# Both MLPs' down-projections computed token by token, summed in SBUF over four blocks, and turned once by PE transposes

## The chip, the core and the metric

The kernel runs on one core of a Trainium2 chip. A core has a matrix engine (TensorE, "PE" in the profile) that multiplies a stationary block of up to 128x128, loaded first, with a moving block of up to 512 columns and writes the sums to banks of PSUM; a vector engine (VectorE, DVE), a scalar engine (ScalarE, ACT), GpSimd (POOL), and a queue engine (SyncE, SP) that issues transfers from device memory. The operands lie in SBUF, 128 partitions wide. Each engine works through its own instructions in order and waits for the others by semaphores.

The metric is the device time of one execution in microseconds, median over the runs shown.

## The reference, cut to what matters

The model is a decoder trunk of two layers over 256 tokens with 2048 features: an attention mixer, an MLP with squared ReLU, and a gate with a per-layer embedding. What the change touches is the MLP of both layers, and through it the residual stream `h` that the gate's norm reads:

```python
hn = rmsnorm(h, mlp_norm_g[i])
h = h + jnp.square(jax.nn.relu(hn @ mlp_w1[i])) @ mlp_w2[i]
gate = jax.nn.sigmoid(rmsnorm(h, ple_norm_g[i]) @ ple_w_gate[i])
h = h + (p[i] @ ple_w_proj[i]) * gate
```

`mlp_w1[i]` is 2048 x 8192 and `mlp_w2[i]` 8192 x 2048, all float32. Every product is made from split numbers: each operand is a rounded part (hi) and the rest (lo), and hi x hi, hi x lo and lo x hi are summed.

## The kernel before

**Layout.** Activations are kept feature-major: tile `x[k]` holds features 128k to 128k+127 on the partitions and the 256 tokens along the free axis; two such tiles are one buffer `xp[j]`. A split activation (`xa`, `h`) is a tile of 512 columns, hi for 256 tokens and then lo for the same tokens.

**Weights.** They stream from device memory in chunks of 128x1024 float32, 512 KB each. For each chunk SyncE issues a load to `raw`, ScalarE casts it to `whi` (L196), VectorE subtracts to make `wlo` (L202). `Program.run` writes the order of all this out by hand, one step a chunk: first loads, casts and subtractions for chunks some steps ahead, then `advance`, which moves every open follow-up generator by one `yield`, and then the matmuls of the chunk. A generator that yields `"tensor"` is resumed behind the chunk's matmuls (`finish_tensor`), so that it can put work of its own on TensorE there. Each engine gets its instructions in just this order.

**The quad (L341).** A chunk of the MLP holds 256 input features times 512 output features. `quad` computes four feature-major output tiles at once, in four PSUM banks. For each of the four and each of the two inner blocks, `mm_tile` (L316) takes 128x128 of weights as the stationary operand: hi weights against the 512 columns of the activation (its hi and lo part together, L318), then lo weights against 256 columns (the hi part, L319). These two are called a pair below; a chunk is 8 pairs. The two halves of a bank have to be added afterwards. Banks come from two rings, "mm" with four single banks and "at" with two double ones, and `parity` alternates between them.

**The token-major unit (L384).** The value projections of both mixers use another form: the activation block is stationary and 512 columns of weights move, once each for hi x hi, lo x hi and hi x lo (L401 to L403). Output is token-major, 128 tokens by 512 features, in two banks, one for each half of the tokens, with no halves to add. A chunk is 12 matmuls of 512 columns.

**The MLP (L452).** The hidden width is cut into four blocks of 2048. For each block `b` four quads (the "up stage", 32 chunks) compute the block's hidden tiles `h`, then four quads (the "down stage", 32 chunks) multiply them with `w2`. After each down quad `done` adds the two halves of its four banks straight into `x[k]`, by two vector additions of 256 columns a tile (`add_to_x`, L433), in every block. In the last block it goes on with `renorm` (L302): split the new `x[k]` for the gate (L289 on ScalarE, L293 on VectorE), square it (L218) and sum the squares (L226) for the gate's norm.

**What follows.** `ple` (L489) alternates a projection quad of one chunk with a gate quad of eight. During the first gate quad, from its fifth chunk on, `Norm.factor` waits for all 16 tiles, sums the squares over partitions by four one-column matmuls (`column`, L234), takes root and inverse, and spreads the result over the partitions by two float32 products of 256 columns (`spread`, L257); the same is done in the first up quad of an MLP for its own norm.

Of the kernel before, what the change touches and what calls it, by code (L numbers as in the profile page):

```python
# [10 lines left out]
F32 = mybir.dt.float32  # L11
# [4 lines left out]
P = 128  # L16
D = 2048
T = 256
KT = D // P
# [9 lines left out]
NFB = 4  # L29
# [7 lines left out]
G_ATTN, G_MLP, G_PLE, G_KV, G_FIN = 0, 2, 4, 6, 7  # L37
# [94 lines left out]
def kernel(ctx: ExitStack, tc: tile.TileContext, a: dict, out: bass.AP):  # L132
    nc = tc.nc
# [11 lines left out]
    cur = {}  # L145
# [10 lines left out]
    def bank():  # L156
        return pspool.tile([P, 512], F32, tag="mm", name="mm", bufs=4)

    def banks2():
        return pspool.tile([P, 2, 512], F32, tag="at", name="at", bufs=2)  # L160
# [4 lines left out]
    xp = [xpool.tile([P, 2 * T], F32, name=f"x{j}") for j in range(KT // 2)]  # L165
# [3 lines left out]
    ident = const.tile([P, P], F32, name="ident")  # L169
# [117 lines left out]
    def split_hi(k, gi):  # L287
        t = xap.tile([P, 2 * T], F32R, tag="xa", name="xa")
        nc.scalar.activation(t[:, :T], x[k], AF.Identity, scale=gains[:, gi, k:k + 1])  # L289
        return t  # L290

    def split_lo(t, k, gi):
        nc.vector.scalar_tensor_tensor(t[:, T:], x[k], gains[:, gi, k:k + 1], f32(t[:, :T]),  # L293
                                       op0=ALU.mult, op1=ALU.subtract)
# [7 lines left out]
    def renorm(k, gi, to, norm):  # L302

        t = split_hi(k, gi)
        s = norm.square(k)
        yield
        split_lo(t, k, gi)
        to[k] = t
        norm.add(s)


    def have(acts, k):
        prog.until(lambda: acts[k] is not None)
        return acts[k]

    def mm_tile(ps, hi, lo, col, rhs, first, last):  # L316

        nc.tensor.matmul(ps, hi[:, col:col + P], rhs, start=first, stop=False)  # L318
        nc.tensor.matmul(ps[:, :T], lo[:, col:col + P], rhs[:, :T], start=False, stop=last)  # L319

    def sum_halves(ps):
        s = tmp.tile([P, T], F32, tag="es", name="es", bufs=4)
        nc.scalar.copy(s, ps[:, :T])  # L323
        t = tmp.tile([P, T], F32, tag="et", name="et", bufs=7)
        nc.vector.tensor_add(t, ps[:, T:], s)  # L325
        return t

    parity = [0]

    def four_banks():  # L330
        parity[0] ^= 1
        if parity[0]:
            return [bank() for _ in range(4)]
        return [p[:, i, :] for p in (banks2(), banks2()) for i in range(2)]

    def delayed(g, n):
        for _ in range(n):
            yield
        yield from g

    def quad(src, nk, acts, done, hooks=None, single_ring=False, late=False):  # L341

        st = []
        for c in range(nk // 2):
            def step(hi, lo, c=c):
                if c == 0:
                    st.extend([bank() for _ in range(4)] if single_ring else four_banks())
                for i in range(2):
                    have(acts, 2 * c + i)
                for f in range(4):  # L350
                    for i in range(2):
                        k = 2 * c + i
                        mm_tile(st[f], hi, lo, i * 512 + f * P, acts[k], k == 0, k == nk - 1)
                if c < nk // 2 - 1:
                    return []
                return [delayed(done(f, st[f]), f // 2 if late else 0) for f in range(4)]
            prog.chunk(src(c), step)
            for fn in (hooks or {}).get(c, ()):
                prog.op(fn)
# [21 lines left out]
                for fn in mid:  # L381
                    prog.op(fn)

    def token_major(src, acts, done, hooks=None, ring=bank):  # L384

        st = []
        for c in range(KT // 2):
            def step(hi, lo, c=c):
                if c == 0:
                    if ring is bank:  # L390
                        st.extend([bank(), bank()])
                    else:
                        b = banks2()
                        st.extend([b[:, 0, :], b[:, 1, :]])
                for i in range(2):
                    k = 2 * c + i
                    xg = have(acts, k)
                    wh, wl = hi[:, i * 512:(i + 1) * 512], lo[:, i * 512:(i + 1) * 512]
                    for j in range(2):
                        xh, xl = xg[:, j * P:(j + 1) * P], xg[:, T + j * P:T + (j + 1) * P]  # L400
                        nc.tensor.matmul(st[j], xh, wh, start=k == 0, stop=False)  # L401
                        nc.tensor.matmul(st[j], xl, wh, start=False, stop=False)  # L402
                        nc.tensor.matmul(st[j], xh, wl, start=False, stop=k == KT - 1)  # L403
                return [done(j, st[j]) for j in range(2)] if c == KT // 2 - 1 else []
            prog.chunk(src(c), step)
            for fn in (hooks or {}).get(c, ()):
                prog.op(fn)
# [20 lines left out]
    def split_to(dst, src):  # L428
        nc.scalar.copy(dst[:, :T], src)
        yield  # L430
        nc.vector.tensor_sub(dst[:, T:], src, f32(dst[:, :T]))

    def add_to_x(k, ps):  # L433
        nc.vector.tensor_add(x[k], ps[:, :T], x[k])
        nc.vector.tensor_add(x[k], ps[:, T:], x[k])
# [14 lines left out]
                prog.op(lambda: parity.__setitem__(0, 1))  # L450

    def mlp(layer, xg, norm, to, norm2):  # L452
        for b in range(NFB):
            h = [None] * 16
            for q in range(4):
                def done(f, ps, q=q, h=h):
                    t = sum_halves(ps)
                    yield
                    while norm.r is None:
                        yield  # L460
                    nc.vector.scalar_tensor_tensor(t, t, 0.0, norm.rb, op0=ALU.max, op1=ALU.mult)
                    yield
                    nc.scalar.activation(t, t, AF.Square)
                    ht = cur["h"].tile([P, 2 * T], F32R, tag="h", name="h", bufs=20)
                    yield from split_to(ht, t)
                    h[4 * q + f] = ht
                base = layer * 128 + (b * 4 + q) * 8
                quad(lambda c, base=base: a["w1"][base + c], KT, xg, done,
                     {4: [norm.factor]} if b == 0 and q == 0 else None, late=True)
            for q in range(4):  # L470
                def done(f, ps, q=q, b=b):
                    k = 4 * q + f
                    add_to_x(k, ps)
                    if b == NFB - 1:
                        yield
                        yield from renorm(k, G_PLE + layer, to, norm2)
                base = layer * 128 + (b * 4 + q) * 8
                quad(lambda c, base=base: a["w2"][base + c], 16, h, done, late=True)

    def load_p(layer, to):  # L480
        for k in range(2):
# [99 lines left out]
    def start_x(k):  # L581
        return split_x(k, G_ATTN, x_a0)
# [22 lines left out]
    def qk_done(h, i, ps):  # L605
        if i == 0:
            qk[h] = cur["A"].tile([P, 6 * T], F32, tag="qk", name="qk", bufs=2)
            ready[h] = 0

        def mark():  # L610
            ready[h] += 1
        yield from to_head(ps, n_a0, qk[h][:, i * T:(i + 1) * T], True, mark)
# [84 lines left out]
    def v_unit(u, hooks=None, ring=bank):  # L697
        token_major(lambda c: a["w_v"][u * 8 + c], x_a0, lambda j, ps: v_done(u, j, ps), hooks, ring)

    hooks = {c: [lambda k=k: start_x(k) for k in (2 * c + 2, 2 * c + 3)] for c in range(7)}  # L700
# [3 lines left out]
    for h in range(HA):  # L704
        for i in range(6):
            single(lambda c, h=h, i=i: a["w_qk"][(h * 6 + i) * 2 + c], x_a0,
                   lambda ps, h=h, i=i: qk_done(h, i, ps),
# [19 lines left out]
    p0, p1 = [None] * 2, [None] * 2  # L727
    prog.op(lambda: load_p(0, p0))
    mlp(0, x_m0, n_m0, x_p0, n_p0)
    ple(0, p0, x_p0, n_p0, x_kv, n_b1, False)  # L730

# [394 lines left out]
    for h in range(HB):  # L1126
# [4 lines left out]
        if h:  # L1131
            prog.op(lambda h=h: b_scores(h - 1))
    hooks = {0: [lambda: b_pv(HB - 4, True), lambda: b_transpose(HB - 3)],
             1: [lambda: b_scores(HB - 1, banks2)],
             2: [lambda: b_pv(HB - 3, True), lambda: b_transpose(HB - 2)],
             4: [lambda: b_pv(HB - 2, True), lambda: b_transpose(HB - 1)],
             5: [lambda: b_pv(HB - 1, True)]}
# [3 lines left out]
    prog.op(lambda: open_pool("h"))  # L1141
    prog.op(lambda: load_p(1, p1))
    mlp(1, x_m1, n_m1, x_p1, n_p1)
    ple(1, p1, x_p1, n_p1, None, n_fin, True)

# [99 lines left out]
```

## Time and profile before

| | us |
|---|---|
| median of 3 runs | 2523.98 (2523.86 to 2524.05) |
| the profiled execution | 2523.56 |
| its span, first to last instruction | 2521.8 |
| a down stage (32 chunks) | 88.75 |
| an up stage that is not the first of its layer | 88.74 |
| TensorE busy in the span | 2502.3 |

Times of a profile are microseconds from the span's start unless a column says ns. PE is TensorE's matmul, PEld its weight load. A line such as `L318 PE MATMUL mm<-h,whi` names a source line, engine, operation, and the tiles written and read; "mm" and "at" are the two rings of banks. Busy time of PE counts overlapping latencies, so the distance between starts says more than a duration. PEclk is the granted clock of TensorE as a share of full speed.

### The profile page before, as it was taken

Reading aid. Unit: us, or ns where it says so; the run is one execution under the profiler, and the core shown is the slowest. Engines: PE = TensorE matmul, PEld = TensorE weight load, DVE = VectorE, ACT = ScalarE, POOL = GpSimd, SP = SyncE. Lnnn points to the kernel's source line nnn. Section 1 sums busy time; section 2 is a strip of 40 time slices with the busy share of each in tenths; the row PEclk is TensorE's granted clock in tenths of the full one; section 3 lists DMA queues with packets and bytes.
Section 4 is the critical chain, followed back from the end, with each engine's and each line's share of the span. In section 5 each row is a group of like instructions: output and inputs, shape, how many; then the busy total and the mean of one; then the engine's idle time right before and its main releaser. Section 6 shows DMA issues by size and latency. Waiting matters only on the chain.

```text
span 2521.8 us, 37917 instructions
## 1 busy us (share of the span) xinstructions
PE 2502.3 (99%) x14399; PEld 2198.0 (87%) x14399; DVE 1719.2 (68%) x3005; ACT 1339.7 (53%) x2146; POOL 10.4 (0%) x24
## 2 busy tenths in 40 slices
PE   9999999999999999999999999999999999999997
PEld 7888888888888888888888889888888888888887
DVE  6766677866566665567787989776656556556777
ACT  6444444554354453455564788655435445445555
POOL 0000000000000000000000000000000000000000
PEclk9999999999999999999999999999999999999999
DMA  7555555566666666566566754456666666666663
GB/s 265 175 177 180 172 164 177 176 187 191 189 189 191 192 187 191 191 190 187 186 198 191 243 159 125 142 189 186 191 191 189 189 190 191 190 189 191 191 185 118
DMA packets 129831, 466.23 MB, mean 185 GB/s; under 512 B 14576, under 2 KB 15600, under 8 KB 129648
## 3 DMA queue, kind: packets, MB, share of 16 engines
q1 hardware_dynamic: 128400, 461.76, 58.7%
q8 instruction: 113, 1.85, 0.3%
q0 software_dynamic: 528, 1.07, 0.2%
q10 hardware_dynamic: 720, 0.98, 0.1%
q14 instruction: 70, 0.57, 0.1%
HBM read 461.65 MB, written 2.10 MB: 184 GB/s over the span
## 4 chain that ended last, share of the span: by engine, by line
PE 99%; DVE 1%; DMA 0%; issue 0%; ACT 0%; SPq 0%; DVEq 0%
PE mm L318 31%; PE at L318 26%; PE mm L319 16%; PE at L319 13%; PE mm L403 1%; PE mm L401 1%; PE mm L402 1%; PE at L401 1%; PE at L402 1%; PE at L403 1%; PE at L1092 0%; PE at L635 0%; PE mm L1116 0%; PE mm L855 0%; PE mm L856 0%; PE mm L688 0%
## 5 line engine op out<-in xcount | busy, mean ns | idle before, releaser
L202 DVE TENSOR_TENSOR wlo<-raw,whi 128x1024 fp32r<-128x1024 f32 (+1 forms) x874 | 1065.1, 1220 | 623.6 <-PE at L319 242.1
L196 ACT CAST whi<-raw 128x1024 fp32r<-128x1024 f32 (+1 forms) x874 | 920.3, 1054 | 914.6 <-PE at L318 407.7
L318 PE MATMUL mm<-xa,whi 128*128 128x512 f32 x2176 | 766.4, 396 | 0.0
L319 PE MATMUL mm<-xa,wlo 128*128 128x256 f32 x2176 | 608.8, 280 | 0.0
L318 PE MATMUL at<-xa,whi 128*128 128x512 f32 x1648 | 573.6, 392 | 0.0
L318 PEld LDWEIGHTS mm<-xa,whi 128*128 128x128 f32 x2176 | 407.9, 187 | 92.6 <-issue 0.4
L319 PE MATMUL at<-xa,wlo 128*128 128x256 f32 x1648 | 461.1, 280 | 0.0
L319 PEld LDWEIGHTS mm<-xa,wlo 128*128 128x128 f32 x2176 | 410.8, 189 | 0.4
L318 PEld LDWEIGHTS at<-xa,whi 128*128 128x128 f32 x1648 | 308.3, 187 | 68.0
L318 PE MATMUL mm<-h,whi 128*128 128x512 f32 x1024 | 355.7, 391 | 0.0
L318 PE MATMUL at<-h,whi 128*128 128x512 f32 x1024 | 355.7, 391 | 0.0
L319 PEld LDWEIGHTS at<-xa,wlo 128*128 128x128 f32 x1648 | 311.3, 189 | 0.1
L319 PE MATMUL mm<-h,wlo 128*128 128x256 f32 x1024 | 286.7, 280 | 0.0
L319 PE MATMUL at<-h,wlo 128*128 128x256 f32 x1024 | 286.7, 280 | 0.0
L318 PEld LDWEIGHTS at<-h,whi 128*128 128x128 f32 x1024 | 191.5, 187 | 42.0
L318 PEld LDWEIGHTS mm<-h,whi 128*128 128x128 f32 x1024 | 191.5, 187 | 42.0
L319 PEld LDWEIGHTS mm<-h,wlo 128*128 128x128 f32 x1024 | 193.5, 189 | 0.0
L319 PEld LDWEIGHTS at<-h,wlo 128*128 128x128 f32 x1024 | 193.5, 189 | 0.0
L325 DVE TENSOR_TENSOR et<-mm,es 128x256 f32<-128x256 f32 x137 | 55.7, 421 | 83.0 <-ACT es L323 80.9
L323 ACT COPY es<-mm 128x256 f32<-128x256 f32 x137 | 48.3, 371 | 67.5 <-PE mm L319 64.6
L325 DVE TENSOR_TENSOR et<-at,es 128x256 f32<-128x256 f32 x103 | 43.4, 422 | 36.7 <-ACT es L323 31.2
L323 ACT COPY es<-at 128x256 f32<-128x256 f32 x103 | 37.7, 370 | 51.8 <-DVE et L325 40.3
(292 smaller groups left out, 2372.3 us busy)
## 6 DMA issues: line engine op xcount, KB each, us to landing
raw<-in_w SPq DMA_DIRECT2D x512, 512.0 KB, 3.5
raw<-in_w_qk SPq DMA_DIRECT2D x96, 512.0 KB, 3.6
raw<-in_w_gate SPq DMA_DIRECT2D x56, 512.0 KB, 3.6
raw<-in_w_kv SPq DMA_DIRECT2D x48, 512.0 KB, 4.2
raw<-in_w_v SPq DMA_DIRECT2D x47, 512.0 KB, 3.6
raw<-in_w_q SPq DMA_DIRECT2D x32, 512.0 KB, 4.3
raw<-in_w_oB SPq DMA_DIRECT2D x32, 512.0 KB, 3.6
raw<-in_w_oA SPq DMA_DIRECT2D x16, 512.0 KB, 3.6
```

The source lines that it names most:

```text
L196: nc.scalar.copy(hi[:, c], t[:, c])
L202: nc.vector.tensor_sub(lo[:, c], t[:, c], f32(hi)[:, c])
L318: nc.tensor.matmul(ps, hi[:, col:col + P], rhs, start=first, stop=False)
L319: nc.tensor.matmul(ps[:, :T], lo[:, col:col + P], rhs[:, :T], start=False, stop=last)
L323: nc.scalar.copy(s, ps[:, :T])
L325: nc.vector.tensor_add(t, ps[:, T:], s)
L401: nc.tensor.matmul(st[j], xh, wh, start=k == 0, stop=False)
L402: nc.tensor.matmul(st[j], xl, wh, start=False, stop=False)
L403: nc.tensor.matmul(st[j], xh, wl, start=False, stop=k == KT - 1)
```

## The change

The down stages become token-major units. For each block and each quarter `q` of the output features a unit multiplies the stationary `h` blocks with the moving weights into two banks. `token_major` gets a parameter `whole`: banks alternate between the two rings, and one follow-up serves both token halves. The follow-up `down` adds the banks to a new token-major tile `y` of 256 x 2048 float32 in SBUF: in block 0 ScalarE copies them there, in blocks 1 to 3 VectorE adds them. In the last block it goes on, one `yield` a chunk: behind the second chunk after the unit, eight PE transposes of 128x128 turn the quarter's columns of `y` into two banks of the other ring; then two additions of 512 columns put them into `xp`, and two rounds of `renorm` follow for two tiles each. The loads, their order and the split of the weights stay as they were. The attention mixers' value units use the same helper as before.

```diff
-    def token_major(src, acts, done, hooks=None, ring=bank):
+    def two_banks(mm):
+        if mm:
+            return [bank(), bank()]
+        b = banks2()
+        return [b[:, 0, :], b[:, 1, :]]
+
+    def token_major(src, acts, done, hooks=None, ring=bank, whole=False):
 
         st = []
         for c in range(KT // 2):
             def step(hi, lo, c=c):
                 if c == 0:
-                    if ring is bank:
-                        st.extend([bank(), bank()])
+                    if whole:
+                        parity[0] ^= 1
+                        st.extend([parity[0], two_banks(parity[0])])
+                        st[:] = st[1] + st[:1]
                     else:
-                        b = banks2()
-                        st.extend([b[:, 0, :], b[:, 1, :]])
+                        st.extend(two_banks(ring is bank))
...
-                return [done(j, st[j]) for j in range(2)] if c == KT // 2 - 1 else []
+                if c < KT // 2 - 1:
+                    return []
+                return [done(*st)] if whole else [done(j, st[j]) for j in range(2)]
...
     def mlp(layer, xg, norm, to, norm2):
+
+        def down(b, q, ps0, ps1, mm):
+            c = slice(q * 512, (q + 1) * 512)
+            if b == q == 0:
+                cur["y"] = cur["h"].tile([P, 2, D], F32, name=f"y{layer}")
+            y = cur["y"]
+            for j, ps in enumerate((ps0, ps1)):
+                if b:
+                    nc.vector.tensor_add(y[:, j, c], ps, y[:, j, c])
+                else:
+                    nc.scalar.copy(y[:, j, c], ps)
+            if b < NFB - 1:
+                return
+            yield
+            yield "tensor"
+            tr = two_banks(not mm)
+            for f in range(4):
+                for j in range(2):
+                    k = 4 * q + f
+                    nc.tensor.transpose(tr[f // 2][:, (f % 2 * 2 + j) * P:(f % 2 * 2 + j + 1) * P],
+                                        y[:, j, k * P:(k + 1) * P], ident)
+            yield
+            for i in range(2):
+                nc.vector.tensor_add(xp[2 * q + i], tr[i], xp[2 * q + i])
+            for i in range(2):
+                yield
+                both = [renorm(4 * q + 2 * i + f, G_PLE + layer, to, norm2) for f in range(2)]
+                for g in both:
+                    next(g)
+                yield
+                for g in both:
+                    next(g, None)
+
         for b in range(NFB):
...
             for q in range(4):
-                def done(f, ps, q=q, b=b):
-                    k = 4 * q + f
-                    add_to_x(k, ps)
-                    if b == NFB - 1:
-                        yield
-                        yield from renorm(k, G_PLE + layer, to, norm2)
                 base = layer * 128 + (b * 4 + q) * 8
-                quad(lambda c, base=base: a["w2"][base + c], 16, h, done, late=True)
+                token_major(lambda c, base=base: a["w2"][base + c], h,
+                            lambda ps0, ps1, mm, b=b, q=q: down(b, q, ps0, ps1, mm), whole=True)
```

In the changed kernel the three matmuls of the token-major unit are lines L408 to L410, and the transposes are L481.

## The prediction

> **What bounds the kernel now.** I read the page's busy times first, then its chain, then the groups of instructions, to see which engine sets the end and which lines it spends its time on.
>
> ```profile
> span 2521.8 us, 37917 instructions
> ...
> PE 2502.3 (99%) x14399; PEld 2198.0 (87%) x14399; DVE 1719.2 (68%) x3005; ACT 1339.7 (53%) x2146; POOL 10.4 (0%) x24
> ...
> PE 99%; DVE 1%; DMA 0%; issue 0%; ACT 0%; SPq 0%; DVEq 0%
> PE mm L318 31%; PE at L318 26%; PE mm L319 16%; PE at L319 13%; PE mm L403 1%; PE mm L401 1%; PE mm L402 1%; PE at L401 1%; PE at L402 1%; PE at L403 1%; PE at L1092 0%; PE at L635 0%; PE mm L1116 0%; PE mm L855 0%; PE mm L856 0%; PE mm L688 0%
> ...
> L318 PE MATMUL mm<-h,whi 128*128 128x512 f32 x1024 | 355.7, 391 | 0.0
> L318 PE MATMUL at<-h,whi 128*128 128x512 f32 x1024 | 355.7, 391 | 0.0
> ```
>
> The end is set by TensorE alone: the chain is 99% PE, 86% of it in the matmul pairs of L318 and L319, and these groups show no idle time before them. The 391 ns are latencies of overlapping matmuls; what counts is how far apart they start. So every term below is a count of matmuls times a distance between starts. The 2 x 1024 groups on h are the 256 chunks that the change rewrites (8 pairs a chunk, 32 chunks in each of 8 down stages). I then took the stretches: a down stage, the up stage behind it, and a token-major value unit of mixer A, which already runs the three matmuls that the down stages will get.
>
> ```profile
> core 0: us, PE busy (x) PEld busy (x) DVE busy (x) ACT busy (x) POOL busy (x), PEclk, DMA share, GB/s
> 581.63:670.38 88.75, 88.75 (x515) 78.25 (x513) 52.90 (x70) 37.27 (x43) 0.00 (x0) 1.00 0.61 191
> 670.38:759.12 88.74, 88.74 (x514) 78.24 (x513) 53.81 (x75) 46.80 (x70) 0.00 (x0) 1.00 0.61 190
> 64.83:86.62 21.79, 21.79 (x98) 18.03 (x97) 18.21 (x40) 8.86 (x11) 0.00 (x0) 1.00 0.50 164
> ```
>
> A stage of 32 chunks takes 88.75 us, 2.773 us a chunk, without a gap and at full clock (counts include neighbours that reach into a window). The eight chunks of the token-major unit take 21.79 us, 2.724 a chunk, at the same clock.
>
> **The change part by part.** *The matmuls.* A chunk had 8 matmuls of 512 columns and 8 of 256; it gets 12 of 512. That is 6144 columns either way, but four instructions fewer. The distances stand in the timeline, fast pairs first, then the end of a token-major unit and the pairs behind it (columns: start, duration, instruction).
>
> ```profile
> 758.08 0.39 PE L318 MATMUL at<-xa,whi 128*128 128x512 f32 x1
> 758.31 0.28 PE L319 MATMUL at<-xa,wlo 128*128 128x256 f32 x1
> 758.43 0.39 PE L318 MATMUL at<-xa,whi 128*128 128x512 f32 x1
> ...
> 759.12 0.39 PE L318 MATMUL mm<-h,whi 128*128 128x512 f32 x1
> ```
> ```profile
> 85.71 0.39 PE L403 MATMUL mm<-wlo,xa 128*128 128x512 f32 x1
> ...
> 86.39 0.39 PE L403 MATMUL mm<-wlo,xa 128*128 128x512 f32 x1
> 86.62 0.39 PE L318 MATMUL mm<-xa,whi 128*128 128x512 f32 x1
> ...
> 86.96 0.40 PE L318 MATMUL mm<-xa,whi 128*128 128x512 f32 x1
> ...
> 87.31 0.40 PE L318 MATMUL mm<-xa,whi 128*128 128x512 f32 x1
> ...
> 87.67 0.40 PE L318 MATMUL mm<-xa,whi 128*128 128x512 f32 x1
> ...
> 88.02 0.40 PE L318 MATMUL mm<-xa,whi 128*128 128x512 f32 x1
> ```
>
> A fast pair takes 0.3467 us (88.75 / 256); three token-major matmuls take 0.68 (85.71 to 86.39), 0.2267 each. A chunk falls from 8 x 0.3467 = 2.773 to 12 x 0.2267 = 2.720, so 256 chunks save 256 x 0.0533 = 13.6 us. The unit's 21.79 is 0.03 above 8 x 2.72: its first matmuls are slower. A later unit, behind a slower stretch of pairs, took 0.06 more than 21.76:
>
> ```profile
> 283.51:305.33 21.82, 12.48 (x32) 5.89 (x32) 1.00 0.65 194
> ```
>
> Eight such entries give back 0.4.
>
> The rule of the Trainium skill, "TensorE: Matmul & The Clock Gate", section "Back-to-back issue gap", that a warm matmul takes its columns over 2.4 GHz plus 2.5 ns, speaks against the change. By it four fewer matmuls are worth 10 ns a chunk, 2.6 us in all (an estimate from that page); the trace disagrees, at 227 ns where the rule has 216 and 347 for a pair where it has 325.
>
> *The transposes.* In the last block of each layer every quarter turns 8 blocks of 128x128, so 64 in all, on PE's path between two chunks. Mixer A has nine of them inside a token-major unit:
>
> ```profile
> 439.85 0.27 PE L663 MATMUL at<-ident,p 128*128 128x128 f32 x1
> 439.95 0.27 PE L664 MATMUL at<-ident,p 128*128 128x128 f32 x1
> ...
> 440.50 0.49 PE L666 MATMUL mm<-ident,p 128*128 128x128 f32 x3
> 440.75 0.47 PE L401 MATMUL mm<-whi,xa 128*128 128x512 f32 x1
> 441.06 0.39 PE L402 MATMUL mm<-whi,xa 128*128 128x512 f32 x1
> ...
> 441.52 0.40 PE L401 MATMUL mm<-whi,xa 128*128 128x512 f32 x1
> ```
>
> From 439.85 to 441.52 are nine transposes and three matmuls: 1.67 - 0.68 = 0.99, or 0.11 each. Eight cost 0.88, with a little unrest behind them 0.9; eight groups cost 7.2 us (bounds 7.0 to 7.7).
>
> *The pairs behind a token-major unit.* This is the term that the diff hides. Above, the pairs after 86.62 start 0.34, 0.35, 0.36, 0.35 apart, not 0.347: the stream falls into a slower rhythm, and stays in it.
>
> ```profile
> core 0: us, PE busy (x) PEld busy (x), PEclk, DMA share, GB/s
> 30.14:55.53 25.39, 25.39 (x72) 13.34 (x71) 1.00 0.68 222
> 86.67:95.10 8.43, 8.43 (x24) 4.32 (x23) 1.00 0.72 254
> 146.60:155.08 8.48, 8.46 (x24) 4.32 (x23) 1.00 0.52 181
> 245.18:253.66 8.48, 8.47 (x24) 4.32 (x23) 1.00 0.53 179
> 305.38:313.86 8.48, 8.47 (x24) 4.32 (x23) 1.00 0.62 186
> ```
>
> These windows hold L318 alone behind the five whole value units of mixer A (two open 0.05 late, to leave a neighbour out). 25.44 / 72 and 8.48 / 24 are both 0.3533 a pair, five times of five, with no return until something else comes between. In the MLP each down stage but the last is followed by an up stage of 256 pairs. Today those follow pairs and run at 0.3466; behind token-major matmuls each should take 256 x 0.0067 = 1.71 us longer, and six of them 10.2 us. Bounds: 0, if the fast rhythm comes back at once, and 10.2. I take 10.2, because the nearest rows agree to the nanosecond and the exit state is the same.
>
> *The end of a layer.* The last quarter's work now takes add, transposes, add, and two rounds of splits: by the generator's steps the last input of the gate is ready seven chunks after the quarter's end instead of four, and is needed in the ninth. This hides behind two chunks, 5.5 us; if the cover went, TensorE would wait 2.8 us a chunk. The last transposes are queued behind the gate's first chunk and wait for the projection's banks, which come free some 2 us into that chunk of 2.8 (an estimate: four copies and an addition of about 0.4 each); it too hides. All of the gate's matmuls are queued behind them. The additions from the transposed banks wait on the vector engine, with the next chunk's subtraction behind them, four chunks early. What shows is the slow rhythm: projection and six chunks of the gate, 7 x 8 pairs x 0.0067 = 0.37 a layer, less 0.05 since the norm's column sums move one chunk later; both layers 0.6 (bounds 0 and 0.8). The two wide products of the norm's spread put the stream right:
>
> ```profile
> 1228.43 0.59 PE L257 MATMUL mm<-diag,ones 128*128 128x256 f32 x2
> 1228.67 0.58 PE L318 MATMUL mm<-pg,whi 128*128 128x512 f32 x1
> ...
> 1229.56 0.39 PE L318 MATMUL mm<-pg,whi 128*128 128x512 f32 x1
> ...
> 1229.90 0.39 PE L318 MATMUL mm<-pg,whi 128*128 128x512 f32 x1
> ```
>
> *Other engines, at nothing.*
>
> ```profile
> L434 DVE TENSOR_TENSOR x<-at,x 128x256 f32<-128x256 f32 x80 | 33.3, 417 | 2.1
> L620 ACT ACTIVATE v<-mm,col x10: 680/690/692, 87.5 to 443.8; 128x512 fp32r<-128x512 f32 x5, 128x512 f32<-128x512 f32 x5
> ```
>
> Per stage 32 additions of 0.42 us go and 8 wide ones of about 0.7 (an estimate, from the ScalarE row of that width) come, so VectorE's 52.9 of 88.75 falls; in block 0 ScalarE gets 8 copies of 0.69, on 37.3 of 88.75. The queue of loads keeps its order; a chunk of 512 KB in 2.72 us asks 193 GB/s, where a stretch above had 254. GpSimd only has its memsets' waits reordered.
>
> **Sum.** -13.6 + 0.4 + 7.2 + 10.2 + 0.6 = +4.8 us. The profiled execution took 2523.56 (span 2521.8 and 1.8 around it), 0.4 below the median 2523.98. On the median: 2528.8, which is 0.19% slower. A difference of 0.2%, 5.05 us, is about what a measurement of this kernel can tell from none, so this counts as no difference, just.
>
> **The rivals.**
> *The slow rhythm does not hold* in the up stages or does not arise in quads. Then the sum is -5.4: 2518.6. For it: no row shows it over more than 72 pairs, and every unit above is followed by mixer A's single-bank work. Against: none of the five stretches left it. 17 in 100; in between, if only some stages have it, 8 in 100 (2520 to 2527).
> *Slower: the slow rhythm outlives the spread* up to the next column sums, by the code 33 chunks in layer 0 and 25 in layer 1: 464 pairs x 0.0067 = 3.1 more, 2531.9. It decides from 37 pairs on (0.25 us). For it, that the spread's phase moves with what precedes it; against it the rows at 1229.56 and 1229.90, 0.34 apart, behind a slow stretch too. 12 in 100.
> *The pace goes by columns alone*, so nothing is saved: +18.4, 2542.4. Against it 21.79 us for the unit where 22.18 would be the pairs' pace. 1 in 100.
> *A transpose costs its duration* of 0.27, not its distance: 64 x 0.16 more, 10.2, 2539. Against it nine started 0.11 apart. 1 in 100. The Trainium skill, "TensorE: Matmul & The Clock Gate", section "Part 4: PE-mode transpose", has about 275 ns for one in a kernel and says that the clock does not rise for it; the trace has that duration, yet not that price, and its clock is 1.00 in the windows quoted.
>
> **How the numbers follow.** My forecast has 61 in 100, with its own range 2527.8 to 2530 from the bounds of the terms; about a third of that lies above 2529.0. Slower: 0.22 of it and the three slower rivals, 0.36. Faster: of the first rival's 17 about 12, since 2518.6 lies only 0.3 beyond the line. The rest, 0.52, is within 0.2%. Leaving the first rival out would leave out nearly 2 in 10 before any tail, so the range takes it in: 2518 to 2532.
>
> **What would show it.** Right: down stages of 87.1 us (89.8 with three groups of transposes), up stages of 90.4 in blocks 1 to 3 and 88.7 in block 0, pairs 0.3533 apart behind a down stage; transposes 0.11 apart in groups of 8; no idle time of PE at L408 or at the gate. Wrong: up stages still at 88.7, or a wait of PE on the last transposes.

## The result

| | kernel before | changed kernel |
|---|---|---|
| median of 22 runs each, us | 2524.19 (2523.31 to 2525.69) | 2528.07 (2527.15 to 2529.55) |
| ratio to before | 1 | 1.0015, 95% interval 1.0009 to 1.0021 |
| profiled span, us | 2521.8 | 2526.6 |

The changed kernel is slower by 3.9 us. That is inside the 0.2% that the prediction called no difference, but over 22 runs the interval of 1.0009 to 1.0021 does tell it from none. The forecast was 2528.8.

The page after: its busy times, its chain, and one of the groups that take the place of L318 on h:

```profile
span 2526.6 us, 35959 instructions
...
PE 2506.8 (99%) x13439; PEld 2156.7 (85%) x13439; DVE 1664.5 (66%) x2813; ACT 1349.4 (53%) x2162; POOL 10.4 (0%) x24
...
PE 99%; DVE 1%; DMA 0%; issue 0%; ACT 0%; SPq 0%; DVEq 0%
...
L408 PE MATMUL mm<-whi,h 128*128 128x512 f32 x512 | 199.4, 390 | 0.0
```

TensorE has 960 matmuls less (4096 gone, 3072 and 64 come), VectorE is lighter by 55 us, and TensorE still sets the end at 99%. The stretches of the first layer show where the time went (first up stage, down, up, down, up, the last down stage, and from there to the end of the norm's spread):

```profile
core 0: us, PE busy (x) PEld busy (x) DVE busy (x) ACT busy (x) POOL busy (x), PEclk, DMA share, GB/s
515.63:582.39 66.76, 66.76 (x387) 58.85 (x385) 41.93 (x61) 38.56 (x63) 0.00 (x0) 1.00 0.54 189
582.39:669.47 87.08, 87.08 (x387) 72.10 (x385) 42.89 (x43) 40.32 (x49) 0.00 (x0) 1.00 0.55 194
669.47:759.91 90.44, 90.44 (x514) 78.48 (x512) 52.05 (x69) 47.76 (x72) 0.00 (x0) 1.00 0.53 187
759.91:846.98 87.07, 87.07 (x387) 72.10 (x386) 46.64 (x49) 37.23 (x44) 0.00 (x0) 1.00 0.56 193
846.98:937.42 90.44, 90.44 (x514) 78.39 (x512) 53.24 (x71) 46.74 (x70) 0.00 (x0) 1.00 0.53 187
1114.92:1204.69 89.77, 89.77 (x411) 74.59 (x410) 58.69 (x78) 46.04 (x68) 0.00 (x0) 1.00 0.53 188
1204.69:1231.32 26.63, 26.63 (x160) 23.43 (x158) 18.70 (x32) 13.77 (x22) 5.04 (x12) 1.00 0.59 200
```

The kernel before has 88.75 for a down stage, 88.74 for an up stage, and for the last stretch:

```profile
1202.86:1228.67 25.81, 25.81 (x152) 22.69 (x151) 17.97 (x34) 13.50 (x22) 2.67 (x7) 1.00 0.65 193
```

A down stage gains 1.67, and an up stage that the change does not touch loses 1.70. Against the kernel before, the clock at 1.00 in both:

| term, both layers | worked out | us | predicted |
|---|---|---|---|
| matmuls of the down stages, entries included | 8 x (87.07 - 88.75) | -13.4 | -13.2 |
| transposes in the last down stage and behind it | 8 x 0.90, from (89.77 - 87.07) / 3 | +7.2 | +7.2 |
| up stages behind a down stage | 6 x (90.44 - 88.74) | +10.2 | +10.2 |
| end of the layer, without its transposes | 2 x (26.63 - 25.81 - 0.90) | -0.2 | +0.6 |
| sum | | +3.8 | +4.8 |

The sum agrees with the medians' 3.9. The two profiled spans differ by 4.8, but 0.75 of that lies ahead of the first MLP: the first up stage after its norm's spread starts at 515.63 here and at 514.88 in the trace before, and the code up to there is the same.

The exit from a down stage, as the prediction read it off mixer A (timeline; start, duration, instruction):

```profile
669.24 0.39 PE L410 MATMUL at<-wlo,h 128*128 128x512 f32 x1
...
669.47 0.39 PE L318 MATMUL mm<-xa,whi 128*128 128x512 f32 x1
...
669.81 0.40 PE L318 MATMUL mm<-xa,whi 128*128 128x512 f32 x1
...
670.16 0.40 PE L318 MATMUL mm<-xa,whi 128*128 128x512 f32 x1
...
670.52 0.40 PE L318 MATMUL mm<-xa,whi 128*128 128x512 f32 x1
...
670.87 0.40 PE L318 MATMUL mm<-xa,whi 128*128 128x512 f32 x1
```

The pairs start 0.34, 0.35, 0.36 and 0.35 apart again, and 90.44 / 256 = 0.3533 is their mean over the whole stage.

### The profile page after: what moved, and what is told of

Read it like the earlier page. It is cut to its first block, busy times and chain, and to the rows that moved or that the text cites. A ratio compares the mean times of both kernels' runs of the same rounds, so it can differ in the third digit from the quotient of the medians.

```text
span 2526.6 us, 35959 instructions
## 1 busy us (share of the span) xinstructions
PE 2506.8 (99%) x13439; PEld 2156.7 (85%) x13439; DVE 1664.5 (66%) x2813; ACT 1349.4 (53%) x2162; POOL 10.4 (0%) x24
## 4 chain that ended last, share of the span: by engine, by line
PE 99%; DVE 1%; DMA 0%; issue 0%; ACT 0%; SPq 0%; DVEq 0%
PE mm L318 22%; PE at L318 17%; PE mm L319 11%; PE at L319 9%; PE mm L408 6%; PE mm L410 6%; PE mm L409 6%; PE at L408 6%; PE at L409 5%; PE at L410 5%; PE at L1129 0%; PE at L672 0%; PE mm L1153 0%; PE mm L892 0%; PE mm L893 0%; PE mm L725 0%
## 5 line engine op out<-in xcount | busy, mean ns | idle before, releaser
L318 PE MATMUL mm<-xa,whi 128*128 128x512 f32 x2176 | 771.8, 399 | 0.0
L319 PE MATMUL mm<-xa,wlo 128*128 128x256 f32 x2176 | 609.5, 280 | 0.0
L318 PE MATMUL at<-xa,whi 128*128 128x512 f32 x1648 | 578.8, 396 | 0.0
L318 PEld LDWEIGHTS mm<-xa,whi 128*128 128x128 f32 x2176 | 408.6, 188 | 97.2 <-issue 0.4
L319 PE MATMUL at<-xa,wlo 128*128 128x256 f32 x1648 | 461.4, 280 | 0.0
L319 PEld LDWEIGHTS mm<-xa,wlo 128*128 128x128 f32 x2176 | 410.7, 189 | 0.7
L318 PEld LDWEIGHTS at<-xa,whi 128*128 128x128 f32 x1648 | 309.0, 188 | 72.7
L319 PEld LDWEIGHTS at<-xa,wlo 128*128 128x128 f32 x1648 | 311.1, 189 | 0.1
L408 PE MATMUL at<-whi,h 128*128 128x512 f32 x512 | 199.5, 390 | 0.0
L408 PE MATMUL mm<-whi,h 128*128 128x512 f32 x512 | 199.4, 390 | 0.0
L409 PE MATMUL mm<-whi,h 128*128 128x512 f32 x512 | 199.3, 389 | 0.0
L410 PE MATMUL mm<-wlo,h 128*128 128x512 f32 x512 | 199.2, 389 | 0.0
L410 PE MATMUL at<-wlo,h 128*128 128x512 f32 x512 | 199.2, 389 | 0.0
L409 PE MATMUL at<-whi,h 128*128 128x512 f32 x512 | 199.2, 389 | 0.0
L410 PEld LDWEIGHTS mm<-wlo,h 128*128 128x128 f32 x512 | 96.1, 188 | 20.0
L408 PEld LDWEIGHTS mm<-whi,h 128*128 128x128 f32 x512 | 96.1, 188 | 20.0
L410 PEld LDWEIGHTS at<-wlo,h 128*128 128x128 f32 x512 | 96.1, 188 | 20.0
L409 PEld LDWEIGHTS at<-whi,h 128*128 128x128 f32 x512 | 96.1, 188 | 19.8
L408 PEld LDWEIGHTS at<-whi,h 128*128 128x128 f32 x512 | 96.1, 188 | 19.8
L409 PEld LDWEIGHTS mm<-whi,h 128*128 128x128 f32 x512 | 96.1, 188 | 19.6
```

## The experiments

Theory R, from the prediction: the slow rhythm is a state of TensorE's own instruction stream. A run of regular 512-column matmuls sets it, and it lasts until some other kind of TensorE work comes between. Theory M, the rival: something else in the new stages slows the up stages, such as the y tile, the banks, the lighter vector engine or the placement of tiles.

**Token-major matmuls in the kernel before (before_tm).** The quads and everything else of the kernel before stay, with 12, 6, 3, 1, 2 and 24 extra matmuls behind six down stages.

```diff
+    def interlude(kind, w, n, xg):
+        ps = bank()
+        for i in range(n):
...
+                nc.tensor.matmul(ps[:, :w], xg[0][:, :P], xg[0][:, :w], start=True, stop=True)
...
                 quad(lambda c, base=base: a["w2"][base + c], 16, h, done, late=True)
+            if b < NFB - 1:
+                prog.op(lambda b=b: interlude(*BETWEEN[layer][b], xg))
```

> The kernel before, with its quads, and behind the down stages of blocks 0 to 2 some float32r matmuls of 512 columns with no use for their output: 12, 6 and 3 of them in layer 0; 1, 2 and 24 in layer 1. No y tile, no transposes, no other change. Theory R: the up stages behind 12 and 24 of them run at 0.3533 a pair and take 90.4 us instead of 88.7; behind 1 to 6 it can go either way; the time grows by 48 x 0.227 = 10.9 us plus 1.7 for each stage that falls into the slow rhythm, at least 3.4, at most 10.2. Theory M: all up stages stay at 88.7 us and the time grows by 10.9 us alone.

Measured: 2545.99 us in one run, 21.8 above the kernel before. The windows below run over the pairs behind the six places and hold only the hi matmul of each pair, which is L319 in this kernel. 512 pairs are an up and a down stage, 256 an up stage, and each window opens 0.05 late. The columns are stretch, length, busy PE, busy weight load, granted clock, DMA share and GB/s.

```profile
674.15:854.99 180.84, 180.84 (x512) 96.01 (x511) 1.00 0.60 183
856.45:1037.29 180.84, 180.84 (x512) 96.02 (x511) 1.00 0.60 184
1038.04:1126.78 88.74, 88.74 (x257) 47.97 (x256) 1.00 0.61 188
1885.41:2062.86 177.45, 177.45 (x512) 95.56 (x511) 1.00 0.61 190
2063.38:2240.83 177.45, 177.45 (x512) 95.81 (x511) 1.00 0.61 190
2246.35:2336.80 90.45, 90.45 (x257) 48.09 (x256) 1.00 0.57 176
```

Behind 12, 6 and 24 matmuls (first, second and last row) the pairs are slow, behind 3, 1 and 2 they are fast. There is no y tile and no transpose here, so M is not needed: twelve matmuls alone turned a fast stream slow, and so did 24. The six and the three have to be read with what stood ahead of them. The six met a stream that was slow already, up to 854.99, and it stayed slow. The three met a slow one too, up to 1037.29, and behind them the pairs are fast, so three of the same matmuls ended the rhythm. The one and the two left a fast stream fast. Where the rhythm was set it did not end with the up stage. It ran on through the quads of the down stage, 512 pairs, 3.4 us a place instead of the 1.7 that the expectation counted. That explains a time above the expected 14.3 to 21.1: 10.9 for the matmuls, 3.4, 3.4 and 3.7 for three slow stretches (the last goes on into the gate), 21.4 in all.

**What clears it (map_a, map_b, map_c).** The changed kernel with eighteen pieces of TensorE work at the six places between a down and an up stage, all into a spare bank:

```diff
+            if kind == "turn":
+                nc.tensor.transpose(ps[:, i % 4 * P:(i % 4 + 1) * P], ident, ident)
+            elif kind == "f32":
+                nc.tensor.matmul(ps[:, :w], ones, xp[0][:, :w], start=True, stop=True)
...
                 token_major(lambda c, base=base: a["w2"][base + c], h,
                             lambda ps0, ps1, mm, b=b, q=q: down(b, q, ps0, ps1, mm), whole=True)
+            if b < NFB - 1:
+                prog.op(lambda b=b: interlude(*BETWEEN[layer][b], xg))
```

> The changed kernel with six different short pieces of TensorE work between a down stage and the up stage behind it, outputs unused: layer 0: one float32 product of 1 column, one transpose of 128x128, one float32 product of 256 columns; layer 1: eight transposes, one float32r product of 256 columns, three of those. Theory R (the slow rhythm is a state of TensorE's own instruction stream, entered from the regular three-matmul stream and left when a float32 product or transposes come between): the up stage behind the 256-column float32 product falls from 90.4 to 88.7 us, that behind the eight transposes too; the single float32r products of 256 columns leave 90.4; the one-column product and the single transpose can go either way. Theory M (something else of the new stages slows the up stages: the y tile, the banks, the lighter vector engine, the placement of tiles): all six stay at 90.4 and the time only grows by the pieces, about 2 us. Under R the time falls by 1.7 us for each stage that recovers, less the pieces.

> As the run before, with six other pieces: layer 0: two float32 products of 1 column, two transposes, one float32 product of 128 columns; layer 1: one float32r product of 128 columns, two float32r products of 256 columns, four transposes. Theory R: the float32 product of 128 columns and the four transposes bring the up stage behind them back to 88.7 us, the float32r products do not; the two short ones can go either way. Theory M: all six stay at 90.4 us.

> Six more pieces, one a place: layer 0: three float32 products of 1 column, one of 64 columns, six transposes; layer 1: one float32 product of 192 columns, three transposes, four float32 products of 1 column. If a longer stop of the float32r stream is what clears the slow rhythm, the 192-column product, the six transposes and the four one-column products clear it (88.7 to 88.9 us) and the 64-column one does not (90.5). If it is a matter of phase, fast and slow are not in the order of the pieces' lengths.

Measured, in one run each: 2526.52, 2527.86 and 2527.49 us. The up stages of the first map (one 1-column product, one transpose, one 256-column product; eight transposes, one and three float32r products):

```profile
669.49:759.97 90.48, 90.48 (x256) 48.03 (x256) 1.00 0.58 186
847.10:937.57 90.47, 90.47 (x256) 48.03 (x256) 1.00 0.59 186
1024.97:1113.86 88.89, 88.89 (x256) 47.80 (x256) 1.00 0.59 189
1873.52:1962.31 88.79, 88.79 (x256) 47.80 (x256) 1.00 0.57 187
2049.55:2139.95 90.40, 90.40 (x256) 47.95 (x256) 1.00 0.58 187
2227.46:2317.86 90.40, 90.40 (x256) 47.94 (x256) 1.00 0.58 186
```

and those of the third (three 1-column products, one of 64, six transposes; one of 192, three transposes, four 1-column products):

```profile
670.79:761.27 90.48, 90.48 (x256) 48.03 (x256) 1.00 0.57 185
848.52:939.00 90.48, 90.48 (x256) 48.02 (x256) 1.00 0.58 186
1026.67:1115.45 88.78, 88.78 (x256) 47.80 (x256) 1.00 0.58 188
1875.44:1964.28 88.84, 88.84 (x256) 47.80 (x256) 1.00 0.59 189
2051.66:2142.15 90.49, 90.49 (x256) 48.03 (x256) 1.00 0.58 186
2230.08:2318.87 88.79, 88.79 (x256) 47.93 (x256) 1.00 0.58 187
```

An up stage takes 88.8 to 88.9 or 90.4 to 90.5 us, with nothing between. The whole 1.7 us turns on what TensorE ran ahead of the stage, so M falls and R's first half holds. Its second half, that another kind of TensorE work ends the rhythm, holds only in part. In the second map only the two 1-column products cleared it (88.79); its expectation missed on the 128-column product and on the four transposes, both at 90.48. In the third map the four pieces that its expectation named came out as a longer stop would have it, but the three 1-column products, which it did not name, do not fit. From the piece's start to the first pair they took 0.59 us and did not clear the rhythm; six transposes took 0.57 and did. Two 1-column products took 0.36 and cleared it; four transposes took 0.35 and did not. So length does not sort fast from slow. The third run's expectation for that case was a matter of phase. What the phase is counted in, none of these runs shows.

The kernel before has such a piece already. The trace lists a float32 product as two matmuls, so the norm's column sums, four matmuls of L234, are two 1-column products, and its spread, L257, is one wide product and not two. The 24 pairs between the sums and the spread in the kernel before, in the first up quad of the first MLP and in the first gate quad behind it (L318 alone, windows opened 0.05 late):

```profile
506.27:514.63 8.36, 8.36 (x24) 4.43 (x24) 1.00 0.57 187
1219.91:1228.43 8.52, 8.52 (x24) 4.43 (x24) 1.00 0.59 174
```

Without the first pair, 0.44 and 0.43 long, they run at 0.347 and 0.354. The stream ahead of the sums was slow in the first case (0.353 a pair) and fast in the second (0.347). So the same two products ended the slow rhythm at one place and set it at the other, and the kind of piece alone does not decide which.

**A version with the reset (reset_wide, reset_col).** The same piece at all six places: one float32 product of 256 columns, or two of one column.

```diff
+BETWEEN = [[('f32', 256, 1), ('f32', 256, 1), ('f32', 256, 1)], [('f32', 256, 1), ('f32', 256, 1), ('f32', 256, 1)]]
```

> The changed kernel with one float32 product of 256 columns (output unused) at each of the six places where an up stage follows a down stage. Theory R: each costs 0.24 us on the path and 0.2 in the first pair behind it, and gives 1.7 back: the up stages take 88.9, the sum is -1.26 us a place, -7.5 in all: 2520.5, which is 3.7 us (0.15%) faster than the kernel before. Theory M would have +1.5 us over the changed kernel.

> The same six places with two float32 products of one column each. In the run with one such place the piece took 0.36 us and the up stage behind it 88.84: -1.24 us a place, -7.4 in all, 2520.6, if each of the six comes out in a fast rhythm. If what follows a short piece depends on the exact moment, some of the six stay slow, each 1.7 us dearer.

Measured: 2520.54 and 2520.71 us, against 2524.29 for the kernel before in the same runs; ratios 0.9985 (0.9976 to 0.9995) and 0.9986 (0.9977 to 0.9995). Both are faster than the kernel before by some 3.7 us and than the changed kernel by some 7.4. The first reset stage of the wide version (the last one reads 88.89 too), and the piece in the timeline (L319 and L320 are the pair here):

```profile
669.53:758.42 88.89, 88.89 (x256) 47.80 (x256) 1.00 0.58 189
```
```profile
669.23 0.59 PE L468 MATMUL mm<-x,ones 128*128 128x256 f32 x2
669.48 0.59 PE L319 MATMUL mm<-xa,whi 128*128 128x512 f32 x1
...
670.02 0.39 PE L319 MATMUL mm<-xa,whi 128*128 128x512 f32 x1
```

A product whose output nothing reads costs 0.24 us and 0.20 in the first pair behind it, and gives 1.7 us back. The up stages of all six places came out alike, at 88.9 in the wide version and 88.8 in the other, so at these places the outcome repeats, phase or not.

**The transposes twice (turn_twice).**

```diff
+                    for _ in range(2):
-                    nc.tensor.transpose(tr[f // 2][:, (f % 2 * 2 + j) * P:(f % 2 * 2 + j + 1) * P],
-                                        y[:, j, k * P:(k + 1) * P], ident)
+                        nc.tensor.transpose(tr[f // 2][:, (f % 2 * 2 + j) * P:(f % 2 * 2 + j + 1) * P],
+                                            y[:, j, k * P:(k + 1) * P], ident)
```

> The changed kernel with each of the 64 PE transposes done twice into the same place, so 64 more. If a transpose costs its distance of 0.11 us on TensorE's path, the time grows by 7.0 us over the changed kernel, to about 2535. If it costs its duration of 0.27, by 17.5, to 2545.6. If the transposes are hidden behind other waits, by less than 2.

Measured: 2535.49 us (ratio to the kernel before 1.0044, 1.0027 to 1.0061), with 2524.23 for the kernel before in those runs: 7.4 above the changed kernel. The first group of the changed kernel, and one of this kernel:

```profile
1142.15 1.03 PE L481 MATMUL at<-ident,y 128*128 128x128 f32 x8
1142.94 0.48 PE L408 MATMUL at<-whi,h 128*128 128x512 f32 x1
```
```profile
1165.94 1.91 PE L482 MATMUL mm<-ident,y 128*128 128x128 f32 x16
1167.60 0.47 PE L408 MATMUL mm<-whi,h 128*128 128x512 f32 x1
```

0.79 us from the first transpose to the next matmul becomes 1.66: 0.87 for eight more, 0.11 each. A transpose costs its distance between starts, and nothing of it is hidden.

**The end of the layer later (late).** The follow-up of the last quarter is held back by two chunks in layer 0 and four in layer 1.

```diff
             if b < NFB - 1:
                 return
+            for _ in range((2, 4)[layer] if q == 3 else 0):
+                yield
             yield
             yield "tensor"
```

> The changed kernel with the follow-up of the last down quarter held back by two more chunks in layer 0 and by four in layer 1. The prediction said that two chunks cover it: in layer 0 TensorE should wait less than 0.5 us, in layer 1 it should stand idle at the gate's last inputs for some 2 to 6 us, two chunks' time. If nothing was near the path, both layers show no wait and the time stays at 2528.1.

Measured: 2536.43 us in one run, 8.4 above the changed kernel. The cover of two chunks that the prediction counted is not there, and what goes first is not the gate's last inputs. The expectation missed the size of the wait in layer 0, and its place in layer 1. In layer 0 TensorE stands still in the middle of the second quarter's projection (timeline; in brackets the wait and what ended it), and then runs at a lower clock (windows):

```profile
1231.93 0.28 PE L319 MATMUL mm<-pg,wlo 128*128 128x256 f32 x1
1235.90 0.80 PE L318 MATMUL mm<-pg,whi 128*128 128x512 f32 x1 [3.69 <-DVE pj L582]
1236.49 0.41 PE L319 MATMUL mm<-pg,wlo 128*128 128x256 f32 x1
```
```profile
1236.00:1241.00 5.00, 5.00 (x20) 4.29 (x21) 2.06 (x4) 1.32 (x2) 0.00 (x0) 0.67 0.30 102
```

Later tiles delay the norm first. Its inverse then sits on VectorE among the first gate quad's sums, and the additions that free the projection's banks sit behind it:

```profile
1232.78 0.42 DVE L325 TENSOR_TENSOR et<-at,es 128x256 f32<-128x256 f32 x1 [0.44 <-ACT es L323]
1233.12 1.22 DVE L202 TENSOR_TENSOR wlo<-raw,whi 128x1024 fp32r<-128x1024 f32 x1
1234.25 0.16 DVE L247 RECIPROCAL sy<-sz 128x2 f32<-128x2 f32 x1
...
1235.03 0.48 DVE L253 TENSOR_SCALAR diag<-ident,col 128x128 f32<-128x128 f32 x2
1235.43 1.08 DVE L582 TENSOR_TENSOR pj<-mm,es 128x256 f32<-128x256 f32 x3
```

In layer 1 the same place cost 2.3 us of waiting. That is not a second point on a scale: there the gate asks for its inputs before the delayed steps are done, and by the code its `have` then moves them on at once. The two rounds of splits start 2.59 us apart on VectorE in layer 1 and 5.55 us in layer 0. The two waits make 6.0 of the 8.4 us; the rest was not taken apart. A delay of one chunk was not tried, so the margin is known only to be under two chunks.

The eight transposes of layer 1, five chunks into the gate in this run, left the rhythm slow. Behind their first pair seven pairs take 2.47 us, 0.353 each (L318 alone, opened 0.05 late):

```profile
2431.91:2434.33 2.42, 2.42 (x8) 1.26 (x8) 1.00 0.06 24
```

The Trainium skill, "TensorE: Matmul & The Clock Gate", section "What's actually happening", says that an idle window of about 3.4 us brings the clock to half. This stop of 3.69 us agrees: behind it a pair's second matmul starts 0.59 us after the first, and the granted clock of the next 5 us is 0.67 in the mean. Behind the stop of 2.31 us in layer 1 the second matmul starts 0.34 us after the first, and the clock stays at 1.00.

## Why the prediction was right, and where it was not

- **The matmuls, right.** Twelve of 512 columns take 2.72 us a chunk with h as with xa: 87.07 us a stage, entry included. With -13.4 for -13.2 the entries were set slightly too dear, and the rival by columns alone falls. The Trainium skill's rule of 2.5 ns a matmul ("TensorE: Matmul & The Clock Gate", section "Back-to-back issue gap") would have made the stage about 88.4, an estimate from that page; the trace disagrees.
- **The transposes, right.** 0.90 a group and 7.2 in all. Doubling them confirmed the price; the rival by duration falls.
- **The up stages, right, and the term that decides the sign.** Six of six ran at 0.3533 a pair from end to end. The rival that the rhythm dies out has nothing for it; it outlasted 512 pairs where nothing came between.
- **The end of the layer, off in size.** The step that failed is "projection and six chunks of the gate" in the slow rhythm, +0.6. Only the projection and the gate's first chunk ran slow, 16 pairs in 5.65 us (1204.68 to 1210.33). The last quarter's transposes stand behind them, and the pairs behind the transposes are fast. The column sums, which set the slow rhythm here in the kernel before, left it fast in the changed kernel. Its windows behind the transposes and behind the column sums (hi matmuls, opened 0.05 late):

```profile
1211.17:1225.08 13.91, 13.91 (x40) 7.43 (x40) 1.00 0.63 211
1225.49:1231.08 5.59, 5.59 (x16) 2.92 (x16) 1.00 0.47 166
```

Without the first pair, 0.43 long in both, the pairs take 0.347 each. So a layer has 16 slow pairs here where the kernel before had 24, which is 0.05 us less. The transposes cost 0.79 and 0.08 in the pair behind them, 0.03 less than the 0.90 of a group. That makes the -0.08 a layer, -0.2 in all. This and the entries make the whole 1.0 between +4.8 and +3.8. The prediction used the spread as a reset, but did not ask the same of the transposes; as eight transposes also left a slow stream slow in the run with the late follow-up, it could not have been sure of it.
- **"This hides behind two chunks", right in the result, wrong in the margin.** No wait shows in the last stretch of the changed kernel. Yet with two chunks more in layer 0 TensorE stood still for 3.69 us, because the norm and the projection's banks come before the gate's last inputs.
- **The rival that ends slower** (the rhythm outlives the spread) did not come: behind the spread the pairs are fast, as before.

## What to carry to other kernels

Where one engine is busy 99% of the time, cost a change by distances between starts, and measure them also in the stage behind the one that is changed: here an untouched stage gave back three quarters of the gain. A rewrite that turns out slower may be one small piece away from a gain; here a product without a use, six times, turned +3.9 us into -3.7. A cover counted in steps holds only for the consumer that was looked at, so every reader of the delayed tile has to be listed.

## What the runs showed of the hardware that was not expected

TensorE's stream of alternating 512- and 256-column float32r matmuls (the rounded type of the split parts, fp32r in the trace) showed two lasting paces in the MLPs, 0.3467 and 0.3533 us a pair, at the same granted clock of 1.00. Twelve and 24 matmuls of 512 columns turned a fast stream slow, and three turned a slow one fast, each at one place of one run. Behind a token-major down stage, float32 products of 192 and 256 columns cleared the slow pace, and those of 64 and 128 did not; two and four of one column did, one and three did not; six and eight transposes did, one to four did not; float32r products of 128 and 256 columns did not. One wide product, or two of one column, cleared it at all six places when put at each of them. No piece is a sure reset elsewhere: eight transposes once left a slow stream slow, and in the kernel before the same two 1-column products turned a slow stream fast in the MLP's first quad and a fast one slow in the gate's. Once set, either pace held for as long as nothing came between: 512 pairs in the slow case, and 2032 in the fast one, from the first MLP's spread at 514.63 to the gate's column sums at 1219.50 in the kernel before. What the state is made of stays open.
